# First memory page and first weight page of a hybrid decoder layer loaded in smaller transfers, issued in turn

## The chip, the cores and the metric

The kernel runs on one core of a Trainium2 chip. The metric is device time of one execution in microseconds (us). Numbers are float32 throughout.

## The reference, cut to what matters

One layer of a decoder: three token mixers on the same normalised input, merged by gates, and a gated MLP behind them. Sequence and model width are 1024, there are 256 memory tokens. What the change touches is the beginning of the third mixer, cross-attention into the memory tokens: normalise the memory, multiply it by one weight to get keys and values.

```
def _memory_cross_attention(q, mem_n, w_kv, g_q, g_k):
    k, v = jnp.split(mem_n @ w_kv, 2, axis=-1)        # mem_n: 256 x 1024, w_kv: 1024 x 1024
    qh = _rmsnorm(_split_heads(q, XA_HEADS), g_q)
    kh = _rmsnorm(_split_heads(k, XA_HEADS), g_k)
    ...
y_xa = _memory_cross_attention(xa_q, _rmsnorm(mem, g_mem[l]), w_mem_kv[l], xa_g_q[l], xa_g_k[l])
```

Everything else (stick-breaking attention, mLSTM, projections, the MLP with its convolution) is as it was.

## The kernel before, in words

The kernel is written with tiles: the code names tiles and instructions, and a planner gives each instruction its place in its engine's queue and puts in the waits. The order on an engine is not always the order of the code. All loads named here are issued by SyncE (SP), on one queue of transfers.

At the start, keys and values of the memory are computed, because their operands are small and the rest needs the whole of x first. A "page" is a tile of 128 partitions x 1024 elements, 512 KB.

- `vec`, the table of all gains and biases, is loaded first (L176).
- `mem_load(j)` (L183) loads memory page `j` of two, in a tile tagged `y`. A page holds four of the eight blocks of 128 model channels, each block 256 tokens wide: a quarter of the page each. ScalarE scales each quarter by its gain into `mg[j]` (L189), a tile tagged `pg`.
- `mem_w(which, b)` (L193) loads weight page `b` of four, for keys (`which` 0) or values (1), in tiles that take the tags `raw`, `whi`, `wlo` in turn. A weight page holds two blocks of 128 channels, 512 columns each: a half of the page each.
- `mem_mm(pm, w, b)` (L214) multiplies weight page `b`: for each of the two groups of 128 tokens and each half of the page one product (L219), so four. In the trace each of these is two weight loads and two matmuls, so eight of each. `mem_mm(pk, wk[0], 0)` is the first work that TensorE gets. It reads quarters 0 and 1 of the first memory page and both halves of the first weight page, in the order (tokens 0, half 0), (tokens 0, half 1), (tokens 1, half 0), (tokens 1, half 1).
- `mem_stats()` (L202) squares both memory pages on ScalarE (L204), adds them up on VectorE (L206, L208) and sums over partitions on TensorE (L211).
- `x_page(1, i)` (L257) loads a quarter of the second half of x, with rows of 512 elements; `x_stats` squares it (L267) and adds it up (L270, L272), `rstd` (L158) and `spread` (L172) make row factors on TensorE, and `x_norm` (L280) normalises. Its results go out by L282, and the first half of x is loaded behind that (L259).

In the code the loads stand in this order: memory page 0, key weight page 0, memory page 1, key weight page 1, two pages of x, key weight page 2, two pages of x, key weight page 3, the small gate weight (`wraw`, L295), then the four value weight pages. The products come next: key pages 0 and 1, `mem_stats`, key pages 2 and 3, then `rstd` of x and the value pages.

Of the kernel before, what the change touches and what calls it, by code (L numbers as in the profile page):

```python
# [18 lines left out]
P = 128  # L19
D = 1024  # L20
S = 1024
HALF = 512
KT = D // P
NMEM = 256
# [18 lines left out]
def tile_hybrid_layer(ctx: ExitStack, tc: tile.TileContext, xT, memT, vecs, w_t, w_n, w_kv, w_if,  # L43
# [4 lines left out]
    nc = tc.nc  # L48
# [11 lines left out]
    def nm(s):  # L60
        uid[0] += 1
        return f"{s}_{uid[0]}"
# [5 lines left out]
    def T(shape, tag, dt=F32, bufs=None):  # L68
        pool = {"mw": mlp, "mst": mlp, "px": late[0], "sx": late[0]}.get(tag, sb)
        return pool.tile(shape, dt, tag=tag, name=nm(tag), bufs=bufs or BUFS[tag])  # L70
# [18 lines left out]
    def bank(tag):  # L89
        if tag in ("pj", "pv"):  # L90
            return ps.tile([P, HALF], F32, tag=tag, name=nm("ps_" + tag), bufs=2)
        if px1 is not None:
            if not spare.get(tag):
                t = two(tag)
                spare[tag] = [t[:, 1], t[:, 0]]
            return spare[tag].pop()
        return psx[0].tile([P, HALF], F32, tag=tag, name=nm("ps_" + tag), bufs=2)
# [4 lines left out]
    def hs(h):  # L102
        return slice(h * HALF, (h + 1) * HALF)
# [18 lines left out]
    def col(i, n=1):  # L122
        return vec[:, i:i + n]
# [56 lines left out]
    mraw = []  # L180
    mg = [page() for _ in range(2)]

    def mem_load(j):  # L183
        t = T([P, S], "y")
        mraw.append(t)
        nc.sync.dma_start(t.rearrange("p (k m) -> p k m", k=4), memT[4 * j:4 * j + 4].rearrange("k p m -> p k m"))
        for i in range(4):
            c = slice(i * NMEM, (i + 1) * NMEM)
            nc.scalar.activation(mg[j][:, c], t[:, c], AF.Copy, scale=col(C_GMEM + 4 * j + i))  # L189

    mtags = itertools.cycle(("raw", "whi", "wlo"))

    def mem_w(which, b):  # L193
        t = T([P, S], next(mtags))
        nc.sync.dma_start(t, w_kv[which, b])
        return t

    gqk = const.tile([P, 1], F32, tag="gqk", name="gqk")
    nc.vector.tensor_mul(gqk, col(C_GQ), col(C_GK))
# [63 lines left out]
    def x_stats(xp):  # L263
        acc = []
        for i in range(4):
            sq = wide()
            nc.scalar.activation(sq, xp[i], AF.Square)  # L267
            acc.append(sq)
            if i:
                nc.vector.tensor_add(acc[0], acc[0], sq)  # L270
        a = acc[0][:, hs(0)]
        nc.vector.tensor_add(a, a, acc[0][:, hs(1)])  # L272
        return a
# [10 lines left out]
    pk, pv = [[bank(t) for _ in range(2)] for t in ("z", "pv")]  # L284
    xp = {0: [], 1: []}
    wk, wv = [], []
    mem_load(0)
    wk.append(mem_w(0, 0))
    mem_load(1)
    for b in range(1, 4):  # L290
        wk.append(mem_w(0, b))
        if b < 3:
            xp[1] += [x_page(1, i) for i in (2 * b - 2, 2 * b - 1)]
# [15 lines left out]
    for b in range(4):  # L309
        wv.append(mem_w(1, b))  # L310
# [184 lines left out]
    a = x_stats(xp[0])  # L495
# [557 lines left out]
    for i in range(3 * KT):  # L1053
        b, n = i // KT, i % KT
# [5 lines left out]
        for h in (1, 0):  # L1060
            p = bank("pj")
# [3 lines left out]
            dst, t = merged[n][:, hs(h)], th[:, hs(h)]  # L1065
# [374 lines left out]
```

## Time and profile before

| | |
|---|---|
| median of 3 runs | 1649.16 us (1648.4 to 1650.76) |
| span of the profiled execution | 1646.8 us |
| profiled execution's own time | not given beside its span; the span is 2.4 us below the median of the runs |
| TensorE busy | 1630.4 us, 99% of the span |
| VectorE, ScalarE, GpSimd busy | 73%, 50%, 6% |
| first matmul | 6.83 us after the span's start |
| mean DMA rate over the span | 129 GB/s |

The profile is one execution taken by the hardware profiler; its times are us from the first instruction unless marked ns. PE is TensorE's matmuls, PEld its weight loads (which run beside matmuls), DVE is VectorE, ACT ScalarE, POOL GpSimd, SP SyncE; a name with a q behind it is that engine's instruction queue. L219 is line 219 of the kernel. `raw<-in_w_kv_dram` reads: tile `raw`, written from `in_w_kv_dram`. In an answer in order of time the first number is the start, the second the length, and in brackets stands the idle time before it with what ended it.

### The profile page before, as it was taken

What the parts mean: (1) busy time and instruction counts of PE and PEld (TensorE: products, weight loads), DVE (VectorE), ACT (ScalarE), POOL (GpSimd) and SP (SyncE); (2) the same over time, 40 slices, a digit from 0 to 9 for tenths busy, and PEclk for the clock granted to TensorE, in tenths of its full rate; (3) what the DMA queues carried; (4) which work ended last, traced back from release to release, by engine and by line L of the source; (5) the groups of instructions that cost most, each with busy time, mean ns of one, the idle gap of its engine ahead of it and who ended that gap; (6) DMA issues with size and microseconds to landing.
All of it is one profiled execution on the core that took longest, in us unless ns stands there. A gap on an engine that the chain in (4) does not pass through costs nothing.

```text
span 1646.8 us, 21125 instructions
## 1 busy us (share of the span) xinstructions
PE 1630.4 (99%) x7911; PEld 1332.1 (81%) x7911; DVE 1210.1 (73%) x1683; ACT 827.9 (50%) x1276; POOL 92.4 (6%) x157
## 2 busy tenths in 40 slices
PE   8999999999999999999999999999999999999999
PEld 4788888887877888888788888788888888888887
DVE  5649888859764766766567658997888777799764
ACT  4557777545554454666322334655555545543431
POOL 1012222020000010100000000000000000000000
PEclk9999999999999999999999999999999999999999
DMA  8411111424324665434854453332222221586132
GB/s 295 154 55 34 39 40 65 140 86 150 125 100 139 197 192 167 135 101 136 282 185 159 137 184 127 108 110 71 77 77 85 98 87 51 173 312 243 43 126 82
DMA packets 96393, 212.68 MB, mean 129 GB/s; under 512 B 12432, under 2 KB 36240, under 8 KB 96292
## 3 DMA queue, kind: packets, MB, share of 16 engines
q1 hardware_dynamic: 96292, 211.35, 38.1%
q8 instruction: 62, 1.02, 0.2%
q14 instruction: 39, 0.32, 0.1%
HBM read 156.71 MB, written 54.61 MB: 128 GB/s over the span
## 4 chain that ended last, share of the span: by engine, by line
PE 90%; DVE 4%; DMA 3%; ACT 2%; issue 1%; SPq 0%; POOLq 0%; ACTq 0%; DVEq 0%
PE ps_pj L142 14%; PE ps_pj L143 14%; PE ps_pj L144 14%; PE ps_pv L142 6%; PE ps_pv L143 6%; PE ps_pv L144 6%; PE ps_tr L142 4%; PE ps_tr L144 4%; PE ps_tr L143 4%; PE ps_z L142 3%; PE ps_z L144 3%; PE ps_z L143 3%; PE ps_pv L450 2%; PE ps_tr L430 2%; PE ps_z L404 1%; PE ps_z L405 1%
## 5 line engine op out<-in xcount | busy, mean ns | idle before, releaser
L143 PE MATMUL ps_pj<-h,whi 128*128 128x512 f32 x624 | 244.2, 391 | 0.9 <-DVE h L130 0.9
L129 ACT ACTIVATE whi<-raw 128x512 fp32r<-128x512 f32 (+1 forms) x111 | 93.1, 839 | 172.3 <-PE ps_pj L143 62.6
L142 PE MATMUL ps_pj<-h,whi 128*128 128x512 f32 x416 | 165.7, 398 | 0.9 <-DVE U L1069 0.6
L142 PE MATMUL ps_pj<-pg,whi 128*128 128x512 f32 x396 | 154.7, 391 | 0.9 <-DVE pg L1067 0.9
L144 PE MATMUL ps_pj<-pg,wlo 128*128 128x512 f32 x376 | 146.5, 390 | 0.0
L143 PEld LDWEIGHTS ps_pj<-h,whi 128*128 128x128 f32 x624 | 117.3, 188 | 25.1 <-DVE h L130 1.8
L144 PE MATMUL ps_pj<-h,wlo 128*128 128x512 f32 x328 | 128.1, 391 | 0.0
L826 DVE SCALAR_TENSOR_TENSOR y<-U,vec,y 128x1023 f32<-128x1023 f32 x88 | 112.5, 1279 | 7.5 <-ACT y L824 7.5
L418 DVE TENSOR_TENSOR_SCAN U<-U 128x512 f32<-128x512 f32 (+3 forms) x96 | 92.7, 1007 | 20.6 <-POOL U L413 17.7
L142 PEld LDWEIGHTS ps_pj<-h,whi 128*128 128x128 f32 x416 | 78.2, 188 | 17.4 <-DVE U L1069 1.3
L142 PEld LDWEIGHTS ps_pj<-pg,whi 128*128 128x128 f32 x396 | 74.3, 188 | 17.2 <-DVE pg L1067 1.4
L130 DVE TENSOR_TENSOR wlo<-raw,whi 128x1024 fp32r<-128x1024 f32 x54 | 66.0, 1222 | 26.5 <-ACT whi L129 26.2
L144 PEld LDWEIGHTS ps_pj<-pg,wlo 128*128 128x128 f32 x376 | 70.6, 188 | 14.9 <-DVE wlo L130 0.3
L143 PE MATMUL ps_pj<-pg,whi 128*128 128x512 f32 x188 | 73.4, 390 | 0.0
L144 PEld LDWEIGHTS ps_pj<-h,wlo 128*128 128x128 f32 x328 | 61.6, 188 | 13.1
L129 ACT ACTIVATE whi<-pg 128x512 fp32r<-128x512 f32 (+1 forms) x46 | 35.3, 769 | 61.2 <-PE ps_pv L143 18.2
L824 ACT ACTIVATE y<-U,vec 128x1024 f32<-128x1024 f32 x44 | 54.6, 1241 | 17.5 <-DVE U L728 16.9
L144 PE MATMUL ps_pj<-h,whi 128*128 128x512 f32 x160 | 62.4, 390 | 0.0
L144 PE MATMUL ps_pv<-pg,wlo 128*128 128x512 f32 x150 | 58.4, 389 | 0.0
L130 DVE TENSOR_TENSOR wlo<-raw,wlo 128x512 fp32r<-128x512 f32 x55 | 37.8, 687 | 22.9 <-ACT wlo L129 22.7
L144 PE MATMUL ps_tr<-pg,wlo 128*128 128x512 f32 x140 | 54.5, 389 | 0.0
L407 ACT ACTIVATE U<-ps_z 128x1024 f32<-128x1024 f32 (+3 forms) x48 | 39.1, 814 | 27.6 <-PE ps_z L405 19.6
(465 smaller groups left out, 4331.6 us busy)
## 6 DMA issues: line engine op xcount, KB each, us to landing
raw<-in_w_t_dram SPq DMA_DIRECT2D x29, 512.0 KB
gate_d<-U SPq DMA_DIRECT2D x24, 512.0 KB
U<-gate_d SPq DMA_DIRECT2D x24, 512.0 KB
act_d<-y SPq DMA_DIRECT2D x22, 512.0 KB
pg<-in_w_t_dram SPq DMA_DIRECT2D x21, 512.0 KB
raw<-in_w_dn_dram SPq DMA_DIRECT2D x18, 512.0 KB
raw<-in_w_o_dram SPq DMA_DIRECT2D x16, 512.0 KB
h<-act_d SPq DMA_DIRECT2D x14, 512.0 KB
```

Source lines behind the costliest of these rows:

```text
L129: nc.scalar.activation(hi, src, AF.Copy)
L130: (eng or nc.vector).tensor_sub(lo, src, hi.bitcast(F32))
L142: nc.tensor.matmul(out, lh, rh, start=start, stop=False, skip_group_check=more)
L143: nc.tensor.matmul(out, lh, rl, start=False, stop=False, skip_group_check=more)
L144: nc.tensor.matmul(out, ll, rh, start=False, stop=stop, skip_group_check=more)
L404: nc.tensor.matmul(z[:, a, :w], qs[a][:, ts(rb)], ks[a][:, c], start=True, stop=False)
L407: nc.scalar.activation(f[:, :, 1:w + 1], z[:, :, :w], AF.Sigmoid, scale=-0.125)
L418: nc.vector.tensor_tensor_scan(f[:, a, 1:w + 1], f[:, a, 1:w + 1], f[:, a, 1:w + 1], 1.0 if o == 0 else f[:, a, 0:1], op0=ALU.mult, op1=AL ...
L430: nc.tensor.transpose(pt[:, a, ts(j)], g[:, a, ts(j)], ident)
L450: nc.tensor.matmul(pv[64 * a:64 * a + 64, ts(rb % 4)], sbv[s // 2][:, s % 2, (2 * p + a) * 64:(2 * p + a + 1) * 64], wt[a][:, ts(j)], star ...
L824: nc.scalar.activation(out, u, AF.Identity, bias=bias, scale=taps[0])
L826: nc.vector.scalar_tensor_tensor(out[:, :S - s], u[:, s:], taps[s], out[:, :S - s], op0=ALU.mult, op1=ALU.add)
```

## The change

The first memory page is loaded in three transfers: quarter 0, quarter 1, and quarters 2 and 3 together. The first key weight page is loaded in two, its two halves, with rows of 512 elements. They are issued in turn: quarter 0, half 0, quarter 1, half 1, quarters 2 and 3. Then the second memory page and all else follow as before. The scaling and the products are the same instructions in the same order of the code.

```
-    def mem_load(j):
+    def mem_part(j, a, b):
+        nc.sync.dma_start(mraw[j][:, a * NMEM:b * NMEM].rearrange("p (k m) -> p k m", k=b - a),
+                          memT[4 * j + a:4 * j + b].rearrange("k p m -> p k m"))
+
+    def mem_load(j, parts=((0, 4),), beside=()):
         t = T([P, S], "y")
         mraw.append(t)
-        nc.sync.dma_start(t.rearrange("p (k m) -> p k m", k=4), memT[4 * j:4 * j + 4].rearrange("k p m -> p k m"))
+        for i, (a, b) in enumerate(parts):
+            mem_part(j, a, b)
+            if i < len(beside):
+                beside[i]()
         for i in range(4):
             c = slice(i * NMEM, (i + 1) * NMEM)
             nc.scalar.activation(mg[j][:, c], t[:, c], AF.Copy, scale=col(C_GMEM + 4 * j + i))
...
+    first_w = T([P, S], next(mtags))
+
+    def mem_w_half(i):
+        nc.sync.dma_start(first_w[:, hs(i)], w_kv[0, 0][:, hs(i)])
...
-    mem_load(0)
-    wk.append(mem_w(0, 0))
+    mem_load(0, ((0, 1), (1, 2), (2, 4)), [lambda: mem_w_half(0), lambda: mem_w_half(1)])
+    wk.append(first_w)
     mem_load(1)
```

## The prediction

> **What bounds the kernel now.** I read the head of the page first, then the TensorE waits. "Waits" columns: who waited for whom, us in total, times, longest.
>
> ```profile
> span 1646.8 us, 21125 instructions
> PE 1630.4 (99%) x7911; PEld 1332.1 (81%) x7911; DVE 1210.1 (73%) x1683; ACT 827.9 (50%) x1276; POOL 92.4 (6%) x157
> ...
> PE ps_z L219 <- ACT pg L189: 6.8, 1, 6.8
> ...
> PE ps_pj L142 <- DVE pg L379: 0.5, 1, 0.5
> ```
>
> TensorE is idle for 1646.8 - 1630.4 = 16.4 us, and 6.8 us of that is one wait: the time before its first matmul, the piece the change touches. An edit that changes only the start cannot bring more than 6.8 us, 0.4% of the span. Behind it the waits show one other in the first 60 us, the 0.5 us one, so a TensorE that starts earlier is earlier from then on as long as its operands are there. Next I read the chain of work that ended last, for the first 60 us (start, us, what):
>
> ```profile
> 1.25 4.15 DMA y<-in_memT_dram
> ...
> 6.83 8.63 PE ps_z L219 x16
> ...
> 28.00 2.06 DVE U L280 x3
> ...
> 39.79 7.89 DMA pg<-in_xT_dram
> ```
>
> The memory page lands at 1.25 + 4.15 = 5.40; TensorE runs the key products; at 28.00 VectorE starts the normalisation (L280), and only behind that the second half of x is loaded (39.79). All of it hangs on TensorE's early stream: what it gains there moves through. The waits name ScalarE as what released the first matmul, and the rows of the start show that this is not so:
>
> ```profile
> 5.49 1.70 ACT L189 ACTIVATE pg<-y,vec 128x256 f32<-128x256 f32 x4 [3.19 <-DMA y<-in_memT_dram]
> ...
> L219 PEldq EVENT_SEMAPHORE  x1: 51/51/51, 6.7 to 6.7; - x1
> ...
> 6.80 0.50 PEld L219 LDWEIGHTS ps_z<-raw,pg 128*128 128x128 f32 x2 [6.80 <-ACT pg L189]
> 7.82 0.34 PEld L219 LDWEIGHTS ps_z<-raw,pg 128*128 128x128 f32 x1 [0.52 <-issue]
> ...
> 9.52 0.34 PEld L219 LDWEIGHTS ps_z<-raw,pg 128*128 128x128 f32 x1 [0.52 <-issue]
> 10.15 0.19 PEld L219 LDWEIGHTS ps_z<-raw,pg 128*128 128x128 f32 x1 [0.29 <-issue]
> ...
> 11.87 3.60 PE L219 MATMUL ps_z<-whi,pg 128*128 128x512 f32 x8
> ```
>
> The first product needs one scaled quarter, ready at 5.49 + 0.49 (an 0.49 us instruction, four in 1.70) = 5.98. It starts 0.8 us later, just after a semaphore event of TensorE at 6.7. The SyncE queue says what landed then:
>
> ```profile
> 0.81 0.38 SPq L176 DMA_DIRECT2D vec<-in_vecs_dram  x1
> 1.25 0.42 SPq L186 DMA_DIRECT2D y<-in_memT_dram  x1
> 1.72 0.50 SPq L195 DMA_DIRECT2D raw<-in_w_kv_dram  x1
> 2.26 0.43 SPq L186 DMA_DIRECT2D y<-in_memT_dram  x1
> ...
> 3.28 0.65 SPq L195 DMA_DIRECT2D wlo<-in_w_kv_dram  x1
> 3.98 2.23 SPq L259 DMA_DIRECT2D pg<-in_xT_dram  x4
> 6.71 0.89 SPq L195 DMA_DIRECT2D raw<-in_w_kv_dram  x1
> ...
> 9.48 0.33 SPq L195 DMA_DIRECT2D whi<-in_w_kv_dram  x1
> ...
> SPq L195 <- DMA raw<-in_w_kv_dram: 0.5, 1, 0.5
> SPq L195 <- DMA whi<-in_w_kv_dram: 0.9, 1, 0.9
> ```
>
> The eleventh transfer (6.71) was held until the third, the first weight page, had landed: 6.71. So the weight page, not the memory page, releases the first matmul. In the same way the thirteenth (9.48) was held until the fifth, the second weight page, had landed. Both waited for the transfer eight places ahead of them.
>
> **The transfers' stream.** Windows: length, busy time of five engines, clock, DMA share, GB/s; below them two sizes, and when later data arrives and is used.
>
> ```profile
> 1.75:3.00 1.25, 0.00 (x0) 0.00 (x0) 0.04 (x1) 0.54 (x2) 1.20 (x2) 1.00 0.61 134
> 3.00:4.00 1.00, 0.00 (x0) 0.00 (x0) 0.62 (x7) 0.00 (x0) 0.38 (x1) 1.00 0.93 302
> 4.00:5.00 1.00, 0.00 (x0) 0.00 (x0) 0.00 (x0) 0.00 (x0) 0.00 (x0) 1.00 1.13 427
> 5.00:6.00 1.00, 0.00 (x0) 0.00 (x0) 0.00 (x0) 0.51 (x2) 0.00 (x0) 1.00 0.91 345
> ...
> 10.00:16.00 6.00, 6.00 (x18) 2.92 (x17) 4.42 (x6) 4.02 (x4) 0.00 (x0) 1.00 1.03 384
> ...
> y<-in_memT_dram SPq DMA_DIRECT2D x2, 512.0 KB
> vec<-in_vecs_dram SPq DMA_DIRECT2D x1, 124.0 KB
> ...
> 7.23 1.06 ACT L204 ACTIVATE y<-y 128x1024 f32<-128x1024 f32 x1
> 8.21 1.71 ACT L189 ACTIVATE pg<-y,vec 128x256 f32<-128x256 f32 x4
> ...
> 12.29 1.15 DVE L208 TENSOR_TENSOR y<-y 128x512 f32<-128x512 f32 x2
> ...
> 15.30 0.50 PE L211 MATMUL ps_tr<-ones,y 128*128 128x1 f32 x4
> ...
> 15.10 1.06 ACT L267 ACTIVATE U<-pg 128x1024 f32<-128x1024 f32 x1 [0.29 <-DMA pg<-in_xT_dram]
> 16.45 1.06 ACT L267 ACTIVATE U<-pg 128x1024 f32<-128x1024 f32 x1 [0.30 <-DMA pg<-in_xT_dram]
> ...
> 18.75 0.19 PEld L219 LDWEIGHTS ps_z<-raw,pg 128*128 128x128 f32 x1 [0.24 <-issue]
> 19.18 3.60 PE L219 MATMUL ps_z<-raw,pg 128*128 128x512 f32 x8
> ```
>
> Bytes moved, summed from the windows: 168 kB by 3.0 us, 470 by 4.0, 897 by 5.0, 1242 by 6.0. In queue order vec is 127 kB and a page 524 kB, so the memory page's last byte moves at 4.43 and the weight page's (1175 kB) at 5.8; they land at 5.40 and 6.71, 0.9 to 1.0 us later.
>
> **The change, part by part.**
>
> *Three more issues on SyncE.* Issues in a row start 0.44 to 0.54 us apart (0.81, 1.25, 1.72, 2.26), so what follows is issued 3 x 0.44 to 3 x 0.54 = 1.3 to 1.6 us later: the second memory page at about 3.6 instead of 2.26. I cost this at nothing. Cover: its turn in the stream comes at 5.8, and from the first page one sees an issue at 1.25 needing at most until 3.0 to flow. Without that cover 1.3 to 1.6 us would be lost on every later page. The other loads (weights, x) move by the same and have the same cover or more; the fourth weight page, held until 6.71, loses some 0.9. It becomes the fourteenth transfer, and eight places ahead of it then stands the last memory piece, which lands at 6.7 by the next step: no new wait.
>
> *Pieces in turn.* The order becomes: memory quarter 0 (131 kB, complete at 258 kB), weight half 0 (520), quarter 1 (651), weight half 1 (913), the other two quarters (1175). On the same curve these bytes are through at 3.3, 4.1, 4.4, 5.0 and 5.8 and land 0.95 later: 4.3, 5.1, 5.4, 6.0, 6.7. The first scaling ends at 4.3 + 0.1 + 0.5 = 4.9, weight half 0 is there at 5.1, so TensorE starts at 5.2 instead of 6.80: 1.6 us sooner. The bounds: nothing, if small pieces land no sooner than the page does now, and 6.80 - 4.9 = 1.9, if only the scaling counts. I take 1.6, nearest to how the first two pages landed. The second product needs half 1 (6.0) and quarter 1 scaled (5.4 + 0.6 = 6.0); TensorE asks for it 1.02 us after its start (6.80 to 7.82), at 6.2. That fits, with 0.2 to spare. The second weight page (9.48) is asked for at 11.44 - 1.6 = 9.8, where the loads run one product ahead of 11.87. That fits too.
>
> *What is late next.* First, the memory statistics (L211): their sum is ready at 12.29 + 1.15 = 13.44 and hangs on the second memory page, which does not land sooner. TensorE would get there at 15.30 - 1.6 = 13.7. It fits. Second, the fourth weight page. It is behind four x pages in the queue. Those land 1.35 us apart (ScalarE takes them up at 15.10 and 16.45), so it lands at about 17.8; no byte ahead of it is removed, so that stays. TensorE now loads it at 18.75, and would at 17.15. It will stand from 17.15 on and load at 17.9; the first product then starts at about 17.9 + 0.1 to fill = 18.03 in place of 19.18. **Of 1.6 us, 1.15 are left.** Behind this page the transfers are no longer the limit, and the chain above moves with TensorE.
>
> *Sum.* 1646.8 - 1.15 = 1645.65 for the span. The span is 2.4 us below the median of the three runs, 1649.16, since a run's time has something around it; the change does not touch that. 1649.16 - 1.15 = 1648.0. The three runs differ by 2.4 us (0.14%); I call 0.2%, 3.3 us, what a measurement of this kernel can tell from no change.
>
> **The rivals.**
>
> *The clock does not warm up sooner.* The granted clock reads 1.00 in every window, but the loads come 0.85 us apart up to 9.52 and 0.43 apart from 10.15, so each early product runs at half speed until about 9.9. I assumed that this stretch moves with the start. If it ends at 9.9 whenever TensorE starts, then from 5.2 to 9.9 about 5.4 of the eight go at 0.85 and the other 2.6 at 0.43: the group ends at 11.0 against 11.87, a gain of 0.85. The fourth weight page is then asked for at 17.9, when it is just there: 1648.3. The Trainium skill, "TensorE: Matmul & The Clock Gate", Part 1, states that the gate watches a free-running window of 3413 ns that does not reset when a kernel starts; by that rule the switch need not move with the start, and runs may differ. No row here shows the window itself.
>
> *No gain.* If a transfer is held up by its slowest DMA engine and not by its bytes, the halves land when the page does now, at 6.7: 1649.2. Against it: the memory and the weight page, of equal bytes, landed 1.31 apart and the x pages 1.35 apart, about what 524 kB take at 384 GB/s (1.37): landings follow the bytes.
>
> *Slower, by the stream.* Small rows may move badly: 1.75 to 3.00 shows 134 GB/s at a share of 0.61, 220 GB/s if full, against 384 later. If the first 1049 kB of pieces went at 220 they would take 4.8 us and not the 3.1 from 2.7 to 5.8: 1.7 us later for everything behind. The fourth weight page would land at 19.5, be loaded at 19.6 and its first product start at 19.73 where it now starts at 19.18: 0.55 us lost, 1649.7. It decides from the point where that page lands after 18.95, that is from 1.15 us of lost stream on. For it: the weight rows become half as long. Against it: x is read in rows of that half length, and 384 GB/s flowed while x was read. The Trainium skill, "DMA: Bandwidth & Descriptors", section Bandwidth, asks for 1 MiB or more per transfer for 75% of the peak; by that rule this split goes the wrong way. Its table was taken on GpSimd's queue, and no run here shows it.
>
> *The order changes.* Instructions do not run in the order of the code: ScalarE squared the first page (7.23, L204) before scaling the second (8.21), which the code has first; and the load of wlo (3.28) went ahead of two x pages. A planner that goes by when things are ready may swap more, far behind the start. One swap costs or brings about one instruction or page, 1.1 to 1.35 us by the rows above; past 0.2% takes three or more the same way. Only 9.6 us of idle is left to win behind the start, while a loss has no such end.
>
> **How the numbers follow.** Forecast (0.9 to 1.6 us gained) 0.47; clock fixed 0.13; no gain 0.10; slower stream 0.07; another order 0.23, of which 0.09 ends faster by over 0.2%, 0.05 within, 0.09 slower. The other cases all lie within 0.2%. So faster 0.09, within 0.82, slower 0.09. The predicted time is 1648.0. The range takes in all cases but the far ends of another order: one swap of 1.35 us and half the spread of the runs (1.2) to either side, 1645.5 to 1650.5.
>
> **What would show it.** Right: the first load of TensorE at 5.0 to 5.4 (the first weight half landed near 5.1), loads evenly spaced into the second group, a wait of 0.5 to 0.8 us for the fourth weight page near 17.2 to 17.9, that product at 18.0, and L280's first at about 26.85. Wrong: a first load past 6.2; the half-speed stretch still ending at 9.9; the fourth weight page landing after 18.7; L280 no earlier though the start is; or TensorE's idle time behind 60 us differing by more than 1 us from before, which would mean another order.

## The result, and the profile after

The changed kernel is slower by a little: 1652.61 us median (1650.19 to 1656.87, 21 runs) against 1649.74 (1647.49 to 1653.43, 21 runs), a ratio of 1.0015 [1.0009, 1.002]. The forecast was 1648.0 with a range up to 1650.5, so it was wrong, and to the wrong side. The profiled execution took 1653.91 us, its span 1652.2.

The head of the page and the TensorE waits of the first 60 us (columns as before):

```profile
span 1652.2 us, 21124 instructions
PE 1633.0 (99%) x7911; PEld 1333.1 (81%) x7911; DVE 1210.2 (73%) x1683; ACT 827.8 (50%) x1276; POOL 88.3 (5%) x157
...
PE ps_z L231 <- DMA raw<-in_w_kv_dram: 5.5, 2, 5.3
PE ps_pj L476 <- DVE pg L382: 2.8, 1, 2.8
```

TensorE is busy 2.6 us longer with the same 7911 matmuls, and a wait of 2.8 us stands where there was none. The first line is the start: 5.3 us where it was 6.8. So the start was won; what was lost behind it is read from the start times of the same matmuls in both traces. I call their difference the lag, after minus before.

First 20 us, weight loads, matmuls and ScalarE's scalings in order of time (ScalarE's last row here, L314 after and L302 before, takes up the small gate weight, which lands right behind the fourth weight page):

```profile
5.24 0.50 PEld L231 LDWEIGHTS ps_z<-raw,pg 128*128 128x128 f32 x2 [5.24 <-issue]
7.49 0.50 PEld L231 LDWEIGHTS ps_z<-raw,pg 128*128 128x128 f32 x2 [1.75 <-issue]
...
12.12 3.67 PE L231 MATMUL ps_z<-whi,pg 128*128 128x512 f32 x8 [1.09 <-ACT pg L196]
16.01 0.60 PE L223 MATMUL ps_tr<-ones,y 128*128 128x1 f32 x4 [0.22 <-DVE y L220]
20.10 1.10 PE L231 MATMUL ps_z<-raw,pg 128*128 128x512 f32 x2
...
3.49 0.51 ACT L196 ACTIVATE pg<-y,vec 128x256 f32<-128x256 f32 x1 [1.20 <-DMA y<-in_memT_dram]
5.48 0.51 ACT L196 ACTIVATE pg<-y,vec 128x256 f32<-128x256 f32 x1 [1.48 <-DMA y<-in_memT_dram]
8.73 0.91 ACT L196 ACTIVATE pg<-y,vec 128x256 f32<-128x256 f32 x2 [2.73 <-DMA y<-in_memT_dram]
20.23 0.35 ACT L314 ACTIVATE pg<-hf 128x32 fp32r<-128x32 f32 x2 [0.48 <-DMA hf<-in_w_if_dram]
```

```profile
17.98 0.35 ACT L302 ACTIVATE pg<-hf 128x32 fp32r<-128x32 f32 x2 [0.47 <-DMA hf<-in_w_if_dram]
```

The wait of 1.09 ahead of 12.12 is put down to ScalarE (L196), but the two quarters that this product needs were scaled by 8.73 + 0.91 = 9.64. SyncE's queue shows what landed:

```profile
12.00 0.33 SPq L202 DMA_DIRECT2D whi<-in_w_kv_dram  x1
...
SPq L202 <- DMA whi<-in_w_kv_dram: 0.9, 1, 0.9
```

As in the kernel before (9.48 there), this issue was held until the second weight page, eight places ahead of it, had landed: 12.00. So TensorE waited for that page.

The lag is -1.56 at the first product, +0.25 at the second weight page (12.12 for 11.87), +0.71 at the statistics (16.01 for 15.30) and +0.92 at the fourth weight page (20.10 for 19.18). From there to 48 us it stays at 1.0. The windows of the first 8 us (before, then after; the last number is GB/s) show why:

```profile
0.00:8.00 8.00, 1.17 (x2) 0.68 (x3) 1.14 (x10) 3.96 (x7) 2.59 (x8) 1.00 0.73 245
```

```profile
0.00:8.00 8.00, 2.53 (x3) 1.00 (x4) 1.14 (x10) 2.50 (x4) 0.70 (x6) 1.00 0.61 174
```

245 x 8 = 1960 kB became 174 x 8 = 1392 kB: the stream of transfers ran slower.

The larger part of the loss comes at 50 us, in work that the change doesn't name. SyncE's queue, before and then after:

```profile
38.51 2.50 SPq L259 DMA_DIRECT2D pg<-in_xT_dram  x4
41.80 0.34 SPq L135 DMA_DIRECT2D raw<-in_w_n_dram  x1
```

```profile
42.00 0.33 SPq L135 DMA_DIRECT2D raw<-in_w_n_dram  x1
42.38 2.43 SPq L271 DMA_DIRECT2D pg<-in_xT_dram  x4
```

L259 (L271 after) loads the first half of x, four transfers; L135 loads a weight page that is wanted later. They have changed places. L135 may only be issued when the tile it overwrites has been read, and the chain of work shows what that costs:

```profile
40.83 1.15 DVE wlo L130
42.00 0.33 SPq L135
42.38 6.84 DMA pg<-in_xT_dram
...
50.79 0.60 ACT pg L380
...
52.11 0.70 DVE pg L382
```

The four x loads stand behind L135, and L135 waits for VectorE (L130) until 41.98. x is asked for 3.9 us later than before (38.51). ScalarE's first row of x (L267 before, then L279 after) shows what that does to the first of the four pages:

```profile
45.52 1.06 ACT L267 ACTIVATE U<-pg 128x1024 f32<-128x1024 f32 x1 [0.86 <-DMA pg<-in_xT_dram]
```

```profile
49.24 1.06 ACT L279 ACTIVATE U<-pg 128x1024 f32<-128x1024 f32 x1 [3.58 <-DMA pg<-in_xT_dram]
```

The page is taken up 3.7 us later, and ScalarE stands idle for 3.58 us ahead of it. TensorE's next products (L476) do not read this half of x at all. They write the tile `ps_pj`, and what stands in it has to be copied out first, by ScalarE (L379, L380) and VectorE (L381, L382). In ScalarE's queue these copies stand behind the square of x's first page (L279), before as after, so the late page holds them up and TensorE with them. TensorE's rows there, and one window (the number before the DMA share is the granted clock):

```profile
52.95 0.45 PE L476 MATMUL ps_pj<-h,pg 128*100 128x512 f32 x1 [2.77 <-DVE pg L382]
...
53.60 0.63 PE L476 MATMUL ps_pj<-h,pg 128*100 128x512 f32 x1
54.03 0.63 PE L477 MATMUL ps_pj<-h,pg 128*100 128x512 f32 x1
...
53.30:56.72 3.42, 3.42 (x10) 2.27 (x9) 2.73 (x4) 3.36 (x7) 0.00 (x0) 0.50 0.18 32
```

Behind the wait the clock is 0.50 from 53.30 to 56.72, and matmuls start 0.43 apart where 0.23 is usual. The lag goes from 1.0 to 3.7 by the wait, to 5.25 by the half clock, and back to 4.44 because the next group (L142), which used to wait 0.5 for VectorE, now finds its operand ready.

### The profile page after: what moved, and what is told of

The parts are those of the page before. It is cut to its first block, busy times and chain, and to the rows that moved or that the text cites. A ratio compares the mean times of both kernels' runs of the same rounds, so it can differ in the third digit from the quotient of the medians.

```text
span 1652.2 us, 21124 instructions
## 1 busy us (share of the span) xinstructions
PE 1633.0 (99%) x7911; PEld 1333.1 (81%) x7911; DVE 1210.2 (73%) x1683; ACT 827.8 (50%) x1276; POOL 88.3 (5%) x157
## 4 chain that ended last, share of the span: by engine, by line
PE 89%; DVE 4%; DMA 3%; ACT 2%; issue 1%; SPq 0%; POOLq 0%; ACTq 0%; DVEq 0%
PE ps_pj L142 14%; PE ps_pj L143 14%; PE ps_pj L144 14%; PE ps_pv L143 6%; PE ps_pv L142 6%; PE ps_pv L144 6%; PE ps_tr L144 4%; PE ps_tr L142 4%; PE ps_tr L143 4%; PE ps_z L142 3%; PE ps_z L143 2%; PE ps_z L144 2%; PE ps_pv L462 2%; PE ps_tr L442 2%; PE ps_z L416 1%; PE ps_z L417 1%
## 5 line engine op out<-in xcount | busy, mean ns | idle before, releaser
L142 PE MATMUL ps_pj<-h,whi 128*128 128x512 f32 x416 | 165.6, 398 | 0.2 <-ACT h L129 0.2
L142 PE MATMUL ps_pj<-pg,whi 128*128 128x512 f32 x396 | 154.8, 391 | 1.5 <-DVE pg L1079 1.5
L142 PEld LDWEIGHTS ps_pj<-h,whi 128*128 128x128 f32 x416 | 78.2, 188 | 16.3 <-ACT h L129 0.8
L142 PEld LDWEIGHTS ps_pj<-pg,whi 128*128 128x128 f32 x396 | 74.4, 188 | 17.8 <-DVE pg L1079 2.3
L130 DVE TENSOR_TENSOR wlo<-raw,whi 128x1024 fp32r<-128x1024 f32 x54 | 66.0, 1222 | 26.4 <-ACT whi L129 26.2
L130 DVE TENSOR_TENSOR wlo<-raw,wlo 128x512 fp32r<-128x512 f32 x55 | 37.8, 687 | 22.6 <-ACT wlo L129 22.4
L143 PE MATMUL ps_pv<-h,whi 128*128 128x512 f32 x136 | 53.0, 389 | 0.0
```

The costliest lines, as they stand in the source:

```text
L130: (eng or nc.vector).tensor_sub(lo, src, hi.bitcast(F32))
L142: nc.tensor.matmul(out, lh, rh, start=start, stop=False, skip_group_check=more)
L143: nc.tensor.matmul(out, lh, rl, start=False, stop=False, skip_group_check=more)
```

## Experiments

The two findings, the slower stream and the changed order, had to be told apart, and each needed its own cause. Each ratio is against the kernel before on the same chip; its mean was 1649.95 to 1650.66 in the sets.

### The order

**after_x_first**: the changed kernel, with the x loads put ahead of the weight page again.

```
-    xp[0] = [x_page(0, i) for i in range(4)]
+    with tc.high_priority(offset=40):
+        xp[0] = [x_page(0, i) for i in range(4)]
```

> The changed kernel, with the four loads of x's first half given priority, so that SyncE issues them ahead of the third value-of-attention weight page again, as before; the small transfers at the start stay. Theory A (the order): of the 4.4 us that the profile of after is late at 54 us, 1.0 comes from the start and 3.4 from x being loaded behind that weight page (a wait of 2.8 us at the gates' matmuls, then 3.4 us at half clock). Then here the wait near 50 is at most 0.8 us, the clock stays at full speed behind the start, TensorE is 0.8 to 1.2 us late at 60 us, and the time is some 1650.7 with before at 1649.7. Rival B (the late start alone brings the stall on, whatever the order): the wait of some 2.8 us is still there and the time is that of after, 1652.6.

Measured: 1649.48 us median, ratio 1.000 [0.9991, 1.0009]; mean 1650.10, against 1652.79 of the changed kernel. SyncE's queue is in the old order:

```profile
39.15 2.40 SPq L271 DMA_DIRECT2D pg<-in_xT_dram  x4
42.45 0.44 SPq L135 DMA_DIRECT2D raw<-in_w_n_dram  x1
```

The lag is -1.6 at the start, +0.65 from 20 to 38 us and +0.13 from 54 to 200 (0.8 to 1.2 was expected at 60). The stream is as slow as in the changed kernel (1480 kB by 8 us), and the time is that of before. So the order carries the loss against before, 2.7 us of means. The early start is lost again by 20 us, to the slow stream and to the eight first products, which take 6.31 us instead of 5.20.

**four_dummies** and **two_dummies**: the kernel before, with its transfers untouched, and four or two matmuls of ones ahead of everything. Four make the planner give every queue the changed kernel's order; two leave it as before.

```
+    for _ in range(4):          # two_dummies: range(2)
+        nc.tensor.matmul(pk[0][:, :P], ones, ones, start=True, stop=True)
```

> The kernel before, all loads whole, with four matmuls of ones put ahead of the first product, in TensorE's idle time before 3 us; their result is overwritten. With them the planner gives every queue exactly the order of after (the third weight page of the next product ahead of x's four loads), save for the small transfers. Theory A (the order alone costs the time): up to 45 us TensorE is within 1 us of before, then it waits 2 to 3 us at the gates' matmuls near 50, with a stretch of half clock behind it in part of the runs; the time is 2 to 3.5 us over before. Rival B (the order costs only together with the small transfers and the late start): no wait over 1.3 us near 50, and a time within 1 us of before.

> The control of the run with four: two matmuls of ones, with which the planner keeps the order of before in every queue. Both theories: the time of before, within 0.1%, a wait of some 0.5 us near 53, and the clock at full speed behind the start.

Measured: four 1651.62, ratio 1.001 [1.0001, 1.0019], mean 1652.01; two 1649.51, ratio 0.9991 [0.9983, 1.0], mean 1649.14. The queue and the wait of four, then the queue of two:

```profile
41.19 0.33 SPq L135 DMA_DIRECT2D raw<-in_w_n_dram  x1
41.58 2.04 SPq L259 DMA_DIRECT2D pg<-in_xT_dram  x4
...
PE ps_pj L466 <- DVE pg L372: 1.7, 1, 1.7
```

```profile
38.79 2.32 SPq L259 DMA_DIRECT2D pg<-in_xT_dram  x4
42.09 0.34 SPq L135 DMA_DIRECT2D raw<-in_w_n_dram  x1
```

In the traces, ScalarE and VectorE run in the changed kernel's order with four, instruction for instruction, and in the order of before with two. Without any change of a transfer, the order alone costs 2.9 us of means between four and two, and 1.9 against the kernel before (1650.12), just short of the 2 to 3.5 that were expected. This also shows that the flip is no property of small transfers: four matmuls, which have no tile in common with x, bring it about. The mean clock of a run tells of half-clock stretches too, since one of 3.4 us takes it from 1.000 to 0.999. It doesn't say where they lie: the changed kernel's trace has another one in its last 1.5 us. It is 0.999 or less in 14 of the changed kernel's 21 runs and in 8 of 11 of four_dummies, in none of 11 of two_dummies and in 2 of 11 of after_x_first. The changed kernel's twelve runs at 0.999 average 1653.1, its two at 0.998 took 1654.1 and 1656.9, and the seven at 1.000 average 1651.4; a stretch of 3.4 us at half speed is worth 1.7. So in a typical run the late x costs its wait and then, two times in three, the clock too. Of these four kernels, the changed one alone has a trace with the half-clock stretch behind this wait. The trace of four_dummies is of a run at 1.000, and for the other runs the place of the stretch is argued, not shown.

**before_x_late**: the kernel before with the x loads made less urgent (the same lines as after_x_first, with `offset=-60`), meant as the exact swap.

> The kernel before with whole transfers, and the four loads of x's first half set back in priority, so that the third weight page of that product is issued ahead of them, as in after. Theory A (the order): the first 38 us are as before, x lands some 2.5 us later than the 47.7 of before, TensorE waits 2 to 3 us near 50 and may run a stretch of 3.4 us at half clock behind it; the time is 2 to 3.5 us over before, 1651.7 to 1653.2. Rival B (the stall needs the late start): no wait over 0.8 us near 50 and no change, 1649.7.

Measured: 1650.47, ratio 0.9999 [0.999, 1.0008]. It wasn't the swap: one x load stayed ahead.

```profile
39.32 0.43 SPq L259 DMA_DIRECT2D pg<-in_xT_dram  x1
42.62 0.33 SPq L135 DMA_DIRECT2D raw<-in_w_n_dram  x1
43.00 1.53 SPq L259 DMA_DIRECT2D pg<-in_xT_dram  x3
...
PE ps_pj L142 <- DVE pg L379: 1.3, 1, 1.3
```

The first x page is in time, so ScalarE takes it up at 45.76, nearly as before, and the copies behind it are not held up. The wait is 1.3 us and comes at another place, the mean clock is 1.000 in all 11 runs, and the time doesn't move. The expected loss of 2 to 3.5 us missed.

### The stream

**mem_parts_only** cuts the memory page alone (the whole weight page stands behind its first part), **w_halves_only** the weight page alone, **tiny_loads** cuts nothing and adds three loads of 8 KB, **parts_apart** has all five pieces, but not in turn. The x loads stay ahead in all four.

```
mem_parts_only:
+    mem_load(0, ((0, 1), (1, 2), (2, 4)), [lambda: nc.sync.dma_start(first_w, w_kv[0, 0])])
w_halves_only:
     mem_load(0)
+    mem_w_half(0)
+    mem_w_half(1)
tiny_loads (behind the first weight page; extra is a tile of its own):
+    for i in range(3):
+        nc.sync.dma_start(extra[:, 2 * i:2 * i + 2], w_if...[:, 2 * i:2 * i + 2])
parts_apart:
+    mem_load(0, ((0, 1), (1, 2), (2, 4)))
+    mem_w_half(0)
+    mem_w_half(1)
```

> The memory page in three parts as in after, the first weight page whole behind the first part, and x first as before. Theory S1 (each further transfer at the start costs the stream about the same): two of the three further transfers are left, so the fourth weight page lands some 1.5 us later than the 17.8 of before, at 19.3, and TensorE is late by some 0.4 us at 30 us; 1650.1. Theory S2 (the weight's half rows slow the stream, the parts of the memory page do not): the fourth weight page lands at 17.8, TensorE starts at about 5.8 and is 1.0 us early at 30 us; 1648.7.

> The memory page whole, the first weight page in its two halves behind it, and x first as before. Theory S1 (each further transfer costs the stream about the same): one of three is left, the fourth weight page lands at about 18.5 and TensorE is some 0.5 us early at 30 us. Theory S2 (the half rows slow the stream): the fourth weight page lands at about 20 as in after, TensorE is 1.0 us late at 30 us; 1650.7.

> The kernel before, whole pages, with three further loads of 8 KB each (128 rows of 64 B, not used) behind the first weight page, and x first. Theory S1 (each further transfer costs the stream about 0.5 us, whatever its bytes): the small gate weight, right behind the fourth weight page, is taken up by ScalarE at about 19.5 in place of 18.0, and TensorE is 0.3 to 0.8 us late at 30 us. Theory S3 (pages cut in pieces flow badly; the number of transfers is free): it is taken up at 17.6 to 18.2 and TensorE is not late by more than the clock's warm-up varies (0.8 us).

> The changed kernel with the same five transfers, but the three memory parts first and the two weight halves behind them; x pinned as in after_x_first. Theory A1 (the cost comes from memory and weight pieces in turn): the stream is as with whole pages, ScalarE takes up the gate weight at 17.6 to 19.0 us. Theory A2 (the cost comes from the number of small transfers): 19.5 to 20.3 as in after_x_first (19.88). The first product starts behind the last weight half, some 6.4 to 6.8, in both; the time lies within 0.1% of before, 1649 to 1651.

**halves_act** (and **halves_act2**, the same once more) issues the two halves from ScalarE's queue. **whole_act** is the kernel before with its uncut first weight page on ScalarE's queue. **page_beside** leaves the five pieces on SyncE's queue and takes the second memory page to ScalarE's.

```
halves_act:
-        nc.sync.dma_start(first_w[:, hs(i)], w_kv[0, 0][:, hs(i)])
+        nc.scalar.dma_start(first_w[:, hs(i)], w_kv[0, 0][:, hs(i)])
whole_act:
+        (nc.scalar if which == b == 0 else nc.sync).dma_start(t, w_kv[which, b])
page_beside, in mem_part:
+        q = nc.scalar if j else nc.sync
```

> The changed kernel with the two weight halves issued from ScalarE's queue, so that SyncE issues two fewer; x pinned as in after_x_first. If SyncE's issuing is what slows the stream (three more issues of 0.45 to 0.54 us), the gate weight comes at 17.6 to 19.0 us as with whole pages. If the pieces themselves slow it, at 19.5 to 20.3. The time within 0.1% of before, 1649 to 1651.

> The same kernel as halves_act once more. Theory Q: 1900 to 2088 kB moved by 8.0 us again (2000 in the first run), first product at 5.5 to 6.0, ScalarE takes up the gate weight at 17.6 to 19.3. Theory P, with the first run a chance: below 1600 kB. Time 1647.5 to 1650.

> The kernel before, whole pages, with the first weight page alone issued from ScalarE's queue, x pinned. It tells whether what halves_act won (mean 1648.4, first product at 5.67, first group in 5.44 us) came from the second queue or from the halves. If from the second queue: a first product before 6.2 here too and a time of about 1648.5. If from the halves: first product at 6.4 to 6.9 and 1649.5 to 1650.5. Bytes by 8.0 us 1960 to 2088 kB in both.

> The changed kernel with its five pieces on SyncE's queue as they were, x pinned, and only the second memory page issued from ScalarE's queue, early, so that a whole page flows beside the pieces. Theory Q (one queue of pieces in turn cannot keep the stream full, but the DMA engines could): the bytes moved by 8.0 us rise from 1392 to 1480 kB (three runs with the pieces on one queue) to 1900 or more, as with whole pages (1960 to 2088). Theory P (pieces of 128 and 256 KB move badly wherever they are): 1550 kB or less. Between the two: no verdict. Time within 0.15% of before, 1647.5 to 1652.

Measured, with the bytes moved by 8.0 us worked out as above from each trace's window of 0 to 8 us:

| kernel | kB by 8 us | first product | gate weight taken up | median, ratio |
|---|---|---|---|---|
| before | 1960 | 6.83 | 17.98 | |
| whole pages in five other traces | 2000 to 2088 | | 17.61 to 19.17 | |
| tiny_loads | 1976 | 7.12 | 18.72 | 1650.15, 0.9998 [0.9988, 1.0007] |
| w_halves_only | 1856 | 6.36 | 18.30 | 1650.13, 1.000 [0.9991, 1.0009] |
| mem_parts_only | 1760 | 6.64 | 18.73 | 1649.08, 0.9992 [0.9983, 1.0001] |
| parts_apart | 1648 | 7.22 | 19.86 | 1650.09, 0.9999 [0.9989, 1.0009] |
| after, after_x_first, warm_pieces (in turn) | 1392, 1480, 1448 | 5.27, 5.22, 6.40 | 20.23, 19.88, 19.72 | see there |
| halves_act | 2000 | 5.67 | 19.26 | 1648.70, 0.9991 [0.9979, 1.0002] |
| halves_act2 | 1952 | 5.58 | 19.61 | 1648.66, 0.9987 [0.9977, 0.9996] |
| whole_act | 1960 | 7.13 | 18.14 | 1650.91, 1.0002 [0.9993, 1.0012] |
| page_beside | 1896 | 6.92 | 18.07 | 1655.43, 1.0021 [1.001, 1.0032] |

The windows that carry the upper and the lower end, halves_act2 and page_beside:

```profile
0.00:8.00 8.00, 2.42 (x3) 1.18 (x4) 1.14 (x10) 2.50 (x4) 2.59 (x8) 1.00 0.75 244
```

```profile
0.00:8.00 8.00, 1.07 (x2) 0.57 (x3) 1.14 (x10) 2.83 (x6) 2.59 (x8) 1.00 0.75 237
```

Three more transfers by themselves don't slow the stream (tiny_loads). More pieces on the one queue go with a slower one: two halves, three parts, all five, all five in turn. The ends of this row are clear; its single steps, from one trace each, are no larger than the 128 kB between two traces of uncut pages (1960 and 2088). The same pieces on two queues don't slow it (halves_act, twice). page_beside came out at 1896 kB, which by its own terms is no verdict; it lies just short of the 1900 set for the queue theory and far from the 1550 of the other. With halves_act it says that the DMA engines could carry more than the one queue of pieces gave them. Why a queue can't is not shown by these runs. It wasn't for want of issues, as the ninth transfer of the changed kernel shows:

```profile
4.66 0.44 SPq L202 DMA_DIRECT2D wlo<-in_w_kv_dram  x1
```

By 5.10, `vec` and five pages' worth had been issued, 127 + 5 x 524 = 2750 kB, twice what had moved by 8.0. The bytes are not all, however. What TensorE waits for is a landing, and the second weight page's can be read from SyncE's queue in every trace as above: 9.09 to 10.25 in the seven with uncut pages, 11.50 to 12.00 with five pieces in turn, 11.65 in parts_apart, and 10.91 and 11.40 in halves_act and halves_act2. So the second queue brings the bytes back, but only part of the landing; what holds it up is not shown either.

The gate weight, on which the expectations had built, is no sharp measure: for uncut pages it moves by 1.5 us from trace to trace, and halves_act2 has it at 19.61 with a full stream. By it parts_apart (19.86) fits the theory of the number of transfers, w_halves_only (18.30) the one that each further transfer costs the same, and mem_parts_only (18.73), tiny_loads (18.72) and halves_act (19.26) lie between their two theories. tiny_loads missed both in another way: TensorE is 1.37 us late at 30 us, where at most 0.8 was expected. Its eight first products took 6.28 us instead of 5.20.

In page_beside the planner put L135 ahead of x once more, though x was marked as urgent, and so it became a third case of the order:

```profile
42.33 0.33 SPq L135 DMA_DIRECT2D raw<-in_w_n_dram  x1
42.72 1.96 SPq L272 DMA_DIRECT2D pg<-in_xT_dram  x4
...
PE ps_pj L477 <- DVE pg L383: 3.0, 1, 3.0
```

Its expectation, 1647.5 to 1652, took the old order for granted and missed: 0.2% slower, with a mean clock of 0.999 or less in 5 of 7 runs.

whole_act starts at 7.13 and takes 1650.91, beyond both of its expected ranges and nearer to that of the halves: two queues alone bring no early start, it takes the pieces as well. halves_act and halves_act2 come nearest to the change as it was meant, and the second run's interval lies just below 1. What gains that is not shown: in their traces the second weight page still lands later than before, and at 60 us the lag is -0.36 in the one trace and +1.09 in the other.

### The clock at the start

**warm_start**: the kernel before, x loads ahead, and 14 matmuls of ones ahead of the first product (28 in the trace). **warm_again** is the same once more; **warm_pieces** is after_x_first with 12.

```
+    for _ in range(14):
+        nc.tensor.matmul(pk[0][:, :P], ones, ones, start=True, stop=True)
```

> The kernel before, whole pages and x first, with fourteen matmuls of ones from about 1.1 to 6 us, so that the clock is up when the first product begins; their result is overwritten. Theory C (the half-speed stretch eats what the start gains): the eight matmuls of the first weight page take some 3.5 us in place of 5 to 6, TensorE reaches the fourth weight page before it has landed at 17.8 and goes on at 18.0, 1.1 us ahead of the 19.18 of before; 0.6 to 1.5 us faster than before. Rival (the clock falls back in the gap before the first product): the first products go at 0.85 us each as before, no change.

> The same kernel as warm_start once more, on this run of the chip. If the gain of 0.24% came from the clock being up at the first product, it repeats: 0.997 to 0.9985 of before, clock up before the first product (by 6.9 us at the latest), the eight first products in 3.6 to 3.8 us. If it was chance of later work: 0.999 to 1.0005.

> The changed kernel's five transfers, x pinned ahead of the weight page as in after_x_first, and twelve matmuls of ones ahead of the first product, so that TensorE's clock is up when the pieces land. Theory A (the pieces slow the stream, and with a warm clock the fourth weight page is what TensorE waits for): ScalarE takes up the gate weight at 19.5 to 20.3 us as in the two kernels with pieces so far (whole pages: 17.6 to 19.0), the 4th weight page's first product starts about 19.8, 0.9 to 1 us later than in warm_start (18.87), so the time is 0.5 to 1 us over warm_start's 1646.9, about 1647.6, still under before. Theory B (a stream that varies from run to run whatever the pieces): gate weight at 17.6 to 19.0, the time within 0.3 us of warm_start, about 1646.8. The first product cannot end earlier for the pieces by more than the first load allows: start at 5.3 instead of 7 either way.

Measured: warm_start 1646.86, ratio 0.9976 [0.9967, 0.9985]; warm_again 1645.94, 0.9972 [0.9961, 0.9984]; warm_pieces 1646.86, 0.9982 [0.9973, 0.9991]. All three beat both kernels. The pin on x alone isn't what does it: tiny_loads and whole_act have it too and stand at 0.9998 and 1.0002. TensorE in warm_start, then in warm_pieces:

```profile
1.12 6.00 PE L288 MATMUL ps_z<-ones 128*128 128x128 f32 x28 [1.12 <-DVE nhalf L119]
6.96 3.60 PE L219 MATMUL ps_z<-raw,pg 128*128 128x512 f32 x8
10.40 3.60 PE L219 MATMUL ps_z<-whi,pg 128*128 128x512 f32 x8
...
18.87 2.38 PE L219 MATMUL ps_z<-raw,pg 128*128 128x512 f32 x5 [0.87 <-DMA raw<-in_w_kv_dram]
```

```profile
11.62 3.67 PE L231 MATMUL ps_z<-whi,pg 128*128 128x512 f32 x8 [1.37 <-ACT pg L196]
...
19.59 1.95 PE L231 MATMUL ps_z<-raw,pg 128*128 128x512 f32 x4 [0.32 <-DMA raw<-in_w_kv_dram]
```

The first eight products take 3.60 us instead of 5.20. So the second weight page is multiplied at 10.40 instead of 11.87, although the first product comes no sooner (6.96). Then the fourth weight page is what TensorE waits for, as the forecast said of any early start. With pieces, it is multiplied 0.7 us later (19.59), and the products of the second page wait 1.37 us for that page, which lands at 11.50 by the same reading: a warm clock makes the slow stream visible, and the earlier first product (6.40 for 6.96) wins nothing. The lag against before at 60 us is -0.70 in warm_start and -0.47 in warm_again; the means are 3.5 and 4.3 us lower, where 0.6 to 1.5 was expected. Most of the gain comes later (-2.0 and -1.75 at 400 us, -2.5 at the end), and from what, these runs don't settle. A changed order of x isn't it, since ScalarE's order is that of before. Other traces move as much behind 200 us (after_x_first from +0.15 to +2.41). So the warm clock is shown for the first products; that it brings the whole gain is not.

## Why the prediction was wrong, point by point

- **Start.** Right: first load at 5.24, forecast 5.2. The first quarter was scaled from 3.49 (forecast: landing at 4.3), the second from 5.48 (5.4).
- **Landing of the later pieces.** Failed. "On the same curve these bytes are through": the curve of whole pages was used for pieces. The second half was loaded at 7.49 (forecast: landing at 6.0, asked for at 6.2), and the last memory part was scaled at 8.73 (forecast: landing at 6.7). "That fits too", of the second weight page, failed most: it landed at 12.00, not at 9.48, and TensorE waited 1.09 for it. "It fits", of the memory statistics, failed with it: their sum was ready at 15.96 instead of 13.44, and TensorE waited 0.2 for it. The rival "slower, by the stream" had the mechanism, the place and nearly the rate: 220 GB/s, and the 1392 kB that moved by 8.0, almost all of them from 1.75 on, are 223 over these 6.25 us. Its price of 0.55 us was too low, the lag at the fourth weight page was 0.92, and so was its chance of 0.07. Together with the clock, this term took the forecast gain and no more: after_x_first has both, and its lag at 60 us is +0.13 where -1.15 was forecast.
- **"I cost this at nothing", the three more issues.** Right as far as shown: three more loads left the stream as it was (tiny_loads). "No new wait" was wrong, but cost nothing: the fourth weight page was issued at 8.72, after waiting 0.2 us for the last memory part, and most of the nine pages ahead of it had still to move.
- **"Small rows may move badly."** The argument for that rival was off. Uncut memory pages have the same rows as the memory pieces, and with the same weight halves on another queue the stream is full. By the Trainium skill's "DMA: Bandwidth & Descriptors", Rules for kernel authors, spreading transfers over several issuing engines brings no bandwidth. For whole pages this case agrees (whole_act 1960 kB by 8 us, before 1960). For the pieces it doesn't: 1952 and 2000 kB with the halves on ScalarE's queue, 1392 to 1480 with all on SyncE's. The measurement decides.
- **The clock.** "I assumed that this stretch moves with the start": failed, and so did the rival that it ends at 9.9. The half-clock stretch at the start ended at 8.93 in the changed kernel, 3.7 us after the first product, and 3.0 to 5.6 us after it over the other traces without warming. The rule of the Trainium skill cited in the prediction, a free-running window of 3413 ns ("TensorE: Matmul & The Clock Gate", Part 1), fits this: the one stretch at 53.30 lasted 3413 ns to the last digit of the clock record, and the full-clock stretches ahead of it, 44373 ns here and 40960 ns in page_beside, are 13 and 12 times 3413.3. In the changed kernel the half-clock stretch ended 1.0 us sooner than before (9.92), though the start was 1.6 us sooner, so it lasted 0.6 us longer.
- **The fourth weight page.** Named rightly as next in line, and it is what bounds the warm kernels. It came later (first product at 20.10, forecast 18.03), by the stream.
- **The order.** This is the step that lost the forecast: its sum took the order of the queues as given, and it put an order change aside as a rival with too low a price. The rival had 0.23, and 0.09 for the slow side, and it said "one swap costs or brings about one instruction or page, 1.1 to 1.35 us". The swap of L135 and x cost 3.4 us in the trace (lag 1.0 to 4.44) and 1.9 to 2.9 us of means. The price left out two things. A queue is served in order, so whoever is put behind a load that waits for a tile inherits that wait, in SyncE's queue and again in ScalarE's: x was asked for 3.9 us later, and the copies that TensorE needs stood behind it. And a wait of nearly 3 us may be followed by 3.4 us of half clock, which cost 1.55 us here (lag 3.7 to 5.25). The range's upper end, one swap and half a spread, fell short for that. In all the forecast was off by 3.8 us of means, -1.15 against +2.6: some 2.7 by the order, the rest by the gain that the stream and the clock took.
- **"Behind this page the transfers are no longer the limit."** Failed with it: x at 49 us was, through ScalarE's queue.

## What to carry to other kernels

When a change shifts a planner's times by even a microsecond, compare the order of every queue before and behind the change with the old one, loads that wait for a tile above all, before believing any sum: pin the order, and only then judge the change. Price a swap in a queue by the wait that the load in front holds, not by the length of one transfer; follow the late load through every queue in which other work stands behind its first use; and add the clock's price where TensorE then idles. A cold start is paid from the first real product on, and matmuls on constants while the first loads are under way took it off here.

## What the runs showed of the hardware

- A wait of TensorE shorter than the clock's window can cost the clock: 2.8 us of waiting in the changed kernel were followed by exactly 3413 ns at 0.50, 3.0 us in page_beside likewise. The Trainium skill, "TensorE: Matmul & The Clock Gate", Part 1, warns of idle gaps above some 3.4 us; these two were shorter.
- Five pieces in turn on one queue moved 1392 to 1480 kB by 8 us where uncut pages moved 1960 to 2088; with a second queue beside it 1896 to 2000. With the two halves on the second queue, the page that TensorE waits for next still landed at 10.91 and 11.40, where uncut pages had it at 9.09 to 10.25.
- Uncut transfers in the same order land up to 1.5 us apart from trace to trace 18 us into the kernel (17.61 to 19.17 over six traces of five kernels), more than the whole gain that was forecast.
